# A hybrid token-mixer layer in split float32: its projections as pairs of token-major 2x2 block products in Strassen's seven-product form

## The chip, the core and the metric

The kernel runs on one core of a Trainium2 chip. The metric is the time of one execution on the device in microseconds (us), the median of three runs. TensorE multiplies (PE in the profile, PEld its weight loads), VectorE (DVE), ScalarE (ACT) and GpSimd (POOL) do the elementwise work, and SyncE (SP) issues the loads and stores.

## What is computed

The input `x` holds 512 tokens of 1024 channels, and there is one layer:

```python
h = rms_norm(x, norm_g)
y_a = spatial_gating_branch(h @ wi[:, A], ...)  # u, v, z: gelu(u) * (Ws layernorm(gelu(v)) + b) * silu(z)
y_b = moba_branch(h @ wi[:, B], ...)            # q, k, v, z: causal softmax attention, QK norm, linear bias
y_c = gla_branch(h @ wi[:, C], ...)             # q, k, v, low rank (16), z: gated linear attention
y_d = short_conv_branch(h @ wi[:, D], ...)      # b, c, x, z: b * conv3(c * x) * silu(z)
for i in range(4):
    gate = sigmoid(h @ w_merge_gate[i] + b_merge_gate[i])
    merged += gate * (y[i] @ w_branch_out[i])
x + merged @ w_out
```

Each of u, v, z, q, k and so on is 512 columns wide (in C, q and k together are). With the four gates of 1024 columns, `h` is multiplied by 22 blocks of [1024, 512]. The four branches are multiplied by [512, 1024] each and the sum by [1024, 1024].

## The kernel before

All large products keep float32 accuracy with two float32r halves of each factor (hi + lo), so a product of two [128 x 128] by [128 x 512] tiles is three matmuls into one PSUM bank (hi·hi, lo·hi, hi·lo). `h` is turned once, at the start, into the channel-major halves `hTh` and `hTl` (8 blocks of 128 channels by 512 tokens), and all of it must be there before the first product ends.

Weights arrive in blocks of 1 MB, [128 partitions x 2048], on SP's queue, in three buffers `raw` (`load`, L124). `split` (L134) makes of each half block (128x1024) a `wh` by an ACT copy (L140) and a `wl` by a DVE subtraction (L141), in three buffers each. `proj_t` (L220) gives channel-major results: for 128 channels 24 matmuls of 512 tokens (8 blocks of 128 rows, three matmuls each, L216 to L218) into one bank, from one split piece. `proj_n` (L231) gives token-major results: 96 matmuls into four banks for 512 columns (L242 to L244), from four pieces. Either way 512 columns of `h @ W` are 96 matmuls and four pieces. A branch's output product (`pb` in `merge`, L627) is 96 matmuls, and so is each half of the last projection.

The mixers (`mix_c`, `mix_b`, `mix_a`) are generators whose steps are written between the products by `run` (L285), at so many steps for every 24 matmuls; the tile framework then orders each engine's instructions by priority, with splits and the emptying of banks raised over the mixers (`PRI`). The order on an engine is fixed when the kernel is built, and each engine works through its own in order. The order of the work: C's projections, B's projections with mixer C beside them, merge of C and A's projections with mixer B beside them, merge of B with mixer A, D, merges of A and D, last projection. `s8` tiles are [128 x 2048] float32 buffers (1 MB) from a pool of 8. The low-rank columns of C take 16 matmuls (L356, L357), and four groups of four transposes each turn mixer C's output (`poT`, L487).

Of the kernel before, what the change touches and what calls it, by code (L numbers as in the profile page):

```python
# [8 lines left out]
F32 = mybir.dt.float32  # L9
# [6 lines left out]
P = 128  # L16
# [19 lines left out]
# ---- the weights as the core reads them: blocks of [128 partitions, 2048], in the order of their use  # L36
def _t_blocks(src, c0, n):
    return [(src, 0, KD, c0 + i, 256) for i in range(0, n, 256)]


def _n_blocks(src, c0):
    return [(src, r, 4, c0, 512) for r in (0, 512)]


def _merge_blocks(i, last):
    out = _t_blocks(("w_merge_gate", i), 0, D) if last else []
    for mq in range(2):
        out.append((("w_branch_out", i), 0, 4, mq * 512, 512))
        if not last:
            out += _t_blocks(("w_merge_gate", i), mq * 512, 512)  # L50
    return out


WI = ("w_in", None)
BLOCKS = (_n_blocks(WI, C_OFF + 512) + _t_blocks(WI, C_OFF, 512) + _t_blocks(WI, CZ_OFF, 512)
          + _n_blocks(WI, B_OFF) + _n_blocks(WI, B_OFF + 512) + _n_blocks(WI, B_OFF + 1024)
          + _t_blocks(WI, B_OFF + 1536, 512) + _merge_blocks(2, False)
          + _n_blocks(WI, 512) + _t_blocks(WI, 0, 512) + _t_blocks(WI, 1024, 512) + _merge_blocks(1, False)
          + [(WI, 0, KD, D_OFF + j * 512 + hf * 256, 256) for hf in range(2) for j in (1, 2, 0, 3)]
          + _merge_blocks(0, False) + _merge_blocks(3, True)  # L60
          + _n_blocks(("w_out", None), 0) + _n_blocks(("w_out", None), 512))
BLOCK_AT = {b: i for i, b in enumerate(BLOCKS)}

V_NG, V_MB, V_GB, V_QG, V_KG, V_OG, V_CW, V_CB, NVEC = 0, 8, 40, 42, 43, 44, 45, 57, 61


def lay_out(a):
    """The inputs in the order the core reads them (moves only)."""
# [3 lines left out]
    for i, ((name, sub), r, k, c, n) in enumerate(BLOCKS):  # L72
        m = a[name][0] if sub is None else a[name][0, sub]
        w[i] = m[r:r + k * P, c:c + n].reshape(k, P, n).transpose(1, 0, 2).reshape(P, k * n)
    vec = np.concatenate([a[n].reshape(-1, P) for n in ("norm_g", "b_merge_gate", "c_gate_b", "b_q_norm_g", "b_k_norm_g",
                                                        "c_out_norm_g", "d_conv_w", "d_conv_b")]).T
# [4 lines left out]
            "sb": a["a_spatial_b"][0].reshape(1, -1),  # L81
# [4 lines left out]
def hybrid_mixers(ctx: ExitStack, tc: tile.TileContext, x2, wts, lr, vec, w2, lnab, sb, swT, o2):  # L86
# [30 lines left out]
    RATE_C, RATE_B, RATE_A = 1.2, 1.5, 0.5  # L117
    WARM = 17
    PRI, FIRST = 3000, 8000

    last = {}

    # ---------------------------------------------------------------- weights
    def load(src, r, k, c, n):  # L124
        """Rows r.., columns c.. of a weight as [P, k, n]."""
        i = BLOCK_AT[src, r, k, c, n]
        raw = wp.tile([P, 2048], F32, tag="raw", name="raw")
        with tc.high_priority(offset=0 if i == 0 else PRI):
            for j in range(2 if i == 0 else 1):
                cs = slice(j * 1024, (j + 1) * 1024) if i == 0 else slice(0, 2048)  # L130
                nc.sync.dma_start(raw[:, cs], wts[i, :, cs])
        return raw.rearrange("p (k c) -> p k c", k=k)

    def split(v, sub=None, pri=PRI, pin=lambda ins: ins):  # L134
        """The two float32r halves of a [P, a, b] piece: v == hi + lo."""
        a, b = v.shape[1], v.shape[2]
        hi = wp.tile([P, 1024], F32R, tag="wh", name="wh")[:, :a * b].rearrange("p (k c) -> p k c", k=a)
        lo = wp.tile([P, 1024], F32R, tag="wl", name="wl")[:, :a * b].rearrange("p (k c) -> p k c", k=a)
        with tc.high_priority(offset=pri):
            pin(nc.scalar.copy(hi, v))  # L140
            last["lo"] = pin((sub or nc.vector).tensor_tensor(lo, v, hi.bitcast(F32), ALU.subtract))  # L141
        return hi, lo
# [18 lines left out]
    with tc.high_priority(offset=FIRST):  # L161
        for half in range(2):
# [5 lines left out]
            if half == 0:  # L168
                nc.sync.dma_start(vcol, vec)
# [61 lines left out]
    def proj_n(src, c0, xh, xl, evac, sub=None):  # L231
        """Columns c0..c0+512 of h @ src, sequence-major; evac(t, psum) for each 128 tokens."""
        banks = [bankA(f"pn{t}") for t in range(NT)]
        for kh in range(2):
            raw = None if first else load(src, 512 * kh, 4, c0, 512)
            for kq in range(2):
# [8 lines left out]
                if (kh, kq) != (1, 1):  # L245
                    yield 24
# [566 lines left out]
```

## Time and profile before

| | us |
|---|---|
| median of three runs (lowest, highest) | 700.26 (698.72, 701.78) |
| profiled execution, first to last instruction (its span) | 696.4 |
| between the span and the median | 3.9 |
| PE busy in the span | 682.4 |
| DVE, ACT, POOL busy | 336.9, 235.8, 118.9 |

An execution's own time is given for the timed runs only; of the profiled one the page gives the span. PE's busy time counts pipelined matmuls whose ends are modelled, so the pace of a stream of matmuls is read from the distance of their starts, and not from the mean length of one.

### The profile page before, as it was taken

What the parts mean: (1) busy time and instruction counts of PE and PEld (TensorE: products, weight loads), DVE (VectorE), ACT (ScalarE), POOL (GpSimd) and SP (SyncE); (2) the same over time, 40 slices, a digit from 0 to 9 for tenths busy, and PEclk for the clock granted to TensorE, in tenths of its full rate; (3) what the DMA queues carried; (4) which work ended last, traced back from release to release, by engine and by line L of the source; (5) the groups of instructions that cost most, each with busy time, mean ns of one, the idle gap of its engine ahead of it and who ended that gap; (6) DMA issues with size and microseconds to landing.
All of it is one profiled execution on the core that took longest, in us unless ns stands there. A gap on an engine that the chain in (4) does not pass through costs nothing.

```text
span 696.4 us, 7927 instructions
## 1 busy us (share of the span) xinstructions
PE 682.4 (98%) x3184; PEld 564.1 (81%) x3184; DVE 336.9 (48%) x487; ACT 235.8 (34%) x360; POOL 118.9 (17%) x141
## 2 busy tenths in 40 slices
PE   6999999999999999999999999999999999999997
PEld 5868778888788788788888888888888888888886
DVE  4426476873483446458554444444542244227711
ACT  5547423332233434344332232223132322224400
POOL 3840223352100000005631111000002211000000
PEclk9999999999999999999999999999999999999999
DMA  8314112223103031123323133223113232332131
GB/s 320 126 66 132 61 60 93 90 92 120 61 17 127 39 121 61 61 91 120 114 78 112 61 121 121 92 89 121 62 71 148 82 122 64 118 100 82 61 106 45
DMA packets 11892, 66.69 MB, mean 96 GB/s; under 512 B 1456, under 2 KB 1616, under 8 KB 4816
## 3 DMA queue, kind: packets, MB, share of 16 engines
q1 hardware_dynamic: 11856, 66.20, 26.9%
q8 instruction: 25, 0.41, 0.2%
q14 instruction: 11, 0.09, 0.0%
HBM read 64.09 MB, written 2.10 MB: 95 GB/s over the span
## 4 chain that ended last, share of the span: by engine, by line
PE 94%; DVE 2%; POOL 1%; DMA 1%; issue 1%; ACT 1%; SPq 0%; POOLq 0%; DVEq 0%
PE pt L217 11%; PE pt L218 11%; PE pt L216 11%; PE pn L242 6%; PE pn L243 6%; PE pgt L217 6%; PE pgt L216 6%; PE pn L244 6%; PE pgt L218 6%; PE pb L217 4%; PE pb L218 4%; PE pb L216 4%; PE pgr L458 2%; PE pob L603 1%; PE psc L577 1%; PE plast L783 1%
## 5 line engine op out<-in xcount | busy, mean ns | idle before, releaser
L141 DVE TENSOR_TENSOR wl<-raw,wh 128x1024 fp32r<-128x1024 f32 x104 | 133.7, 1285 | 207.5 <-ACT wh L140 192.3
L140 ACT CAST wh<-raw 128x1024 fp32r<-128x1024 f32 x108 | 113.3, 1049 | 294.0 <-PE pt L217 125.2
L216 PE MATMUL pt<-hTh,wh 128*128 128x512 f32 x352 | 137.9, 392 | 0.0
L217 PE MATMUL pt<-hTl,wh 128*128 128x512 f32 x352 | 137.2, 390 | 0.0
L218 PE MATMUL pt<-hTh,wl 128*128 128x512 f32 x352 | 137.1, 390 | 0.0
L216 PEld LDWEIGHTS pt<-hTh,wh 128*128 128x128 f32 x352 | 66.1, 188 | 14.4 <-issue 0.8
L218 PEld LDWEIGHTS pt<-hTh,wl 128*128 128x128 f32 x352 | 66.1, 188 | 13.7
L217 PEld LDWEIGHTS pt<-hTl,wh 128*128 128x128 f32 x352 | 66.1, 188 | 13.5
L216 PE MATMUL pgt<-hTh,wh 128*128 128x512 f32 x192 | 75.1, 391 | 0.0
L217 PE MATMUL pgt<-hTl,wh 128*128 128x512 f32 x192 | 74.8, 390 | 0.0
L218 PE MATMUL pgt<-hTh,wl 128*128 128x512 f32 x192 | 74.7, 389 | 0.0
L242 PE MATMUL pn<-wh,hTh 128*128 128x512 f32 x160 | 64.0, 401 | 0.0
L243 PE MATMUL pn<-wh,hTl 128*128 128x512 f32 x160 | 62.8, 392 | 0.0
L244 PE MATMUL pn<-wl,hTh 128*128 128x512 f32 x160 | 62.5, 391 | 0.0
L642 POOL TENSOR_TENSOR acc<-acc,gate 128x512 f32<-128x512 f32 x16 | 24.5, 1531 | 175.4 <-DVE gate L640 175.4
L449 POOL TENSOR_TENSOR qb<-e,qk 64x256 f32<-64x256 f32 x28 | 29.3, 1047 | 80.7 <-ACT e L444 44.5
L218 PEld LDWEIGHTS pgt<-hTh,wl 128*128 128x128 f32 x192 | 36.0, 188 | 7.5
L216 PEld LDWEIGHTS pgt<-hTh,wh 128*128 128x128 f32 x192 | 36.0, 188 | 7.4
L217 PEld LDWEIGHTS pgt<-hTl,wh 128*128 128x128 f32 x192 | 36.1, 188 | 7.4
L244 PEld LDWEIGHTS pn<-wl,hTh 128*128 128x128 f32 x160 | 30.2, 189 | 6.3
L242 PEld LDWEIGHTS pn<-wh,hTh 128*128 128x128 f32 x160 | 30.3, 189 | 6.0 <-DVE hTl L197 0.2
L243 PEld LDWEIGHTS pn<-wh,hTl 128*128 128x128 f32 x160 | 30.2, 189 | 5.7
(213 smaller groups left out, 912.8 us busy)
## 6 DMA issues: line engine op xcount, KB each, us to landing
raw<-in_w_dram SPq DMA_DIRECT2D x55, 1024.0 KB, 4.8
x<-in_x_dram SPq DMA_DIRECT2D x4, 512.0 KB, 4.9
xr<-in_x_dram SPq DMA_DIRECT2D x8, 256.0 KB, 3.5
out_dram<-xr SPq DMA_DIRECT2D x8, 256.0 KB, 2.1
raw<-in_w_dram SPq DMA_DIRECT2D x2, 512.0 KB, 8.5
lnb<-in_lnab_dram SPq DMA_DIRECT2D x1, 512.0 KB, 3.7
wsT<-in_swT_dram SPq DMA_DIRECT2D x1, 256.0 KB, 10.3
abias<-in_sb_dram SPq DMA_DIRECT2D x1, 256.0 KB, 5.0
```

What stands on the lines that cost most here:

```text
L140: pin(nc.scalar.copy(hi, v))
L141: last["lo"] = pin((sub or nc.vector).tensor_tensor(lo, v, hi.bitcast(F32), ALU.subtract))
L216: nc.tensor.matmul(ps, hi[:, k, ch], xh[:, k, :], start=(k == 0), stop=False)
L217: nc.tensor.matmul(ps, hi[:, k, ch], xl[:, k, :], start=False, stop=False)
L218: nc.tensor.matmul(ps, lo[:, k, ch], xh[:, k, :], start=False, stop=(k == kt - 1))
L242: nc.tensor.matmul(banks[t], xh[k][:, ts], hi[:, kk, :], start=(k == 0), stop=False)
L243: nc.tensor.matmul(banks[t], xl[k][:, ts], hi[:, kk, :], start=False, stop=False)
L244: nc.tensor.matmul(banks[t], xh[k][:, ts], lo[:, kk, :], start=False, stop=(k == KD - 1))
L449: nc.gpsimd.tensor_tensor(qm[hp, a].rearrange("p c (n h) -> p (c n) h", h=hh), ev[hp, :, hh:], qv[hp, :, hh:], ALU.mult)
L458: nc.tensor.matmul(pgv[:, :, c, :], e[:, c * P:(c + 1) * P], qm[:, :, c, :], start=True, stop=True)
L577: nc.tensor.matmul(psc[:, :n], qT[:, i, h * P:(h + 1) * P], kT[:, :i + 1, h * P:(h + 1) * P], start=True, stop=True)
L642: nc.gpsimd.tensor_tensor(accs[m], accs[m], g, ALU.add)
```

## The change

The 22 blocks `h @ W` are taken in 11 pairs. A pair has 1024 columns: `h` is seen as four blocks of [256 tokens x 512 channels] (A11, A12, A21, A22) and the pair's weights as four blocks of [512 rows x 512 columns], C11 and C21 of the first member and C12 and C22 of the second. `superblock` computes the four result blocks from seven block products in place of eight (Strassen's form with shared sums), each of 24 matmuls (2 groups of 128 tokens, 4 blocks of 128 channels, 3 matmuls). The products' left factors are A11, A12, A22 and four sums S1 to S4, which are made once at the start, on POOL, and split into halves. The right factors are C11, C21, C22 and four sums of weights: a block is added onto the buffer that holds another one by a DMA that accumulates (`add`), issued from POOL, once both pieces of what was in the buffer have been split. The parts that several results share are copied or subtracted out of the banks into `snap` tiles, and a result is formed from a bank and such a tile as it is emptied (`value`, and `silu2` and `gelu2` on top of it).

All results are token-major now. What must be channel-major is turned by groups of four transposes (`flip`): q and k of C, the outputs of mixers A and B, D's product before its convolution and its gate after it, and the merged sum before the last projection. The gates come ahead of the merges that use them, are written to DRAM and read back (`gd`, `gate_of`); so is A's `v` (`vd`). Their bias is added inside the superblock, on POOL and DVE. C's low-rank columns take 40 matmuls of 256 columns. Branch outputs are multiplied token-major, still 96 matmuls each. There are four buffers for `wh` and for `wl`, still three for `raw`, six `s8`. The first product starts from the first two of four token tiles.

The core of the diff, with the new functions:

```diff
-    BLOCKS: _n_blocks and _t_blocks of each projection, _merge_blocks
+BLOCKS = (_quad(WI, CQK, CV) + _quad(WI, CZ_OFF, AV)
+          + [b for i in (2, 1) for b in _quad(("w_merge_gate", i), 0, 512)]
+          + _quad(WI, BQ, BK) + _quad(WI, BV, BZ)
+          + [(("w_branch_out", 2), 0, c) for c in (0, 512)]
+          + _quad(("w_merge_gate", 0), 0, 512) + _quad(WI, AU, AZ)
+          + [(("w_branch_out", 1), 0, c) for c in (0, 512)]
+          + _quad(WI, DC, DX) + _quad(WI, DB, DZ)
+          + [(("w_branch_out", 0), 0, c) for c in (0, 512)]
+          + _quad(("w_merge_gate", 3), 0, 512)
+          + [(("w_branch_out", 3), 0, c) for c in (0, 512)]
+          + _quad(WO, 0, 512))
...
+    def add(raw, src, r, c):
+        with tc.high_priority(offset=PRI):
+            nc.gpsimd.dma_start(raw, wts[BLOCK_AT[src, r, c]], accum_op=ALU.add)
...
+        normed(0)
+        normed(1)
+        pieces1 = [split1(v4(raw1)[:, 0:2, :], 0, nc.gpsimd, pin)]
+        for blk, k0 in ((A11, 0), (A12, 4)):
+            for k in range(4):
+                p = px(0, k0 + k)
+                pin(nc.scalar.activation(blk[0][:, k, :], p, AF.Copy, scale=gk(k0 + k)))
...
+            if k0 == 0:
+                pieces1.append(split1(v4(raw1)[:, 2:4, :], 0, nc.gpsimd, pin))
+                normed(2)
+        normed(3)
...
+    def summed(blk, name, a, b, op):
+        f = s8(f"f_{name}")[:, :1024].rearrange("p (k s) -> p k s", k=4)
+        nc.gpsimd.tensor_tensor(f, a, b, op)
+        nc.scalar.copy(blk[0], f)
+        nc.vector.tensor_tensor(blk[1], f, blk[0].bitcast(F32), ALU.subtract)
+        return f
+    with tc.high_priority(offset=FIRST - 1000):
+        f1 = summed(S1, "s1", h1[:, 0:4, :], h1[:, 4:8, :], ALU.subtract)
+        for q, blk in ((0, A11), (1, A12)):
+            nc.gpsimd.tensor_tensor(h0[:, 4 * q:4 * q + 4, :], blk[0].bitcast(F32), blk[1].bitcast(F32), ALU.add)
+        f2 = summed(S2, "s2", f1, h0[:, 0:4, :], ALU.subtract)
+        summed(S4, "s4", h0[:, 4:8, :], f2, ALU.add)
+        summed(S3, "s3", h0[:, 0:4, :], h1[:, 0:4, :], ALU.subtract)
...
+    def superblock(sa, ca, sb, cb, ev, bias=None, pieces=None, raw=None):
+        c11, c21, c12, c22 = (sa, 0, ca), (sa, 512, ca), (sb, 0, cb), (sb, 512, cb)
+        def product(lhs, pcs, banks, start, after):
+            for j in range(2):
+                js = slice(j * P, (j + 1) * P)
+                for p, (hi, lo) in enumerate(pcs):
+                    for kk in range(2):
+                        k = 2 * p + kk
+                        three(banks[j], lhs[0][:, k, js], lhs[1][:, k, js], hi[:, kk, :], lo[:, kk, :],
+                              start and k == 0, k == 3)
+                emptied(after, j)
+                yield 12
...
+        r1 = raw if raw is not None else fetch(*c11)
+        yield from product(A11, pieces or split(r1), a, True, after1)
+        r3 = fetch(*c21)
+        yield from product(A12, split(r3), a, False, lambda j: ev(j, 0, a[j], ...))
+        add(r1, *c12)
+        yield from product(S1, split(r1), d, True, after5)
+        r2 = fetch(*c22)
+        add(r1, *c22)
+        yield from product(S4, split(r2), d, False, after3)
+        yield from product(S2, split(r1), b, True, lambda j: ev(j, 1, b[j], v[j], ALU.subtract))
+        add(r2, *c12)
+        yield from product(S3, split(r2), b, False, lambda j: ev(2 + j, 1, b[j], s15[j], ALU.subtract))
+        add(r1, *c21)
+        yield from product(A22, split(r1), b, False, lambda j: ev(2 + j, 0, b[j], sp1[j], ALU.add))
...
+    def flip(y, name):
+        pT = bankB(name)
+        for h in range(H):
+            nc.tensor.transpose(pT[:, h * P:(h + 1) * P], y[:, h * P:(h + 1) * P], ident)
+        return pT
...
+    run(chain(superblock(WI, CZ_OFF, WI, AV, ev_zv), gates(2), gates(1)), mixing, RATE_C)
...
+    qT, kT = v4(s8("qT")), v4(s8("kT"))
+    run(superblock(WI, BQ, WI, BK, ev_qk))
```

## Rows read from the trace of the kernel before

**Rows 1.** The page's head, busy times, chain by engine, and load queue.

```profile
span 696.4 us, 7927 instructions
PE 682.4 (98%) x3184; PEld 564.1 (81%) x3184; DVE 336.9 (48%) x487; ACT 235.8 (34%) x360; POOL 118.9 (17%) x141
...
q1 hardware_dynamic: 11856, 66.20, 26.9%
...
PE 94%; DVE 2%; POOL 1%; DMA 1%; issue 1%; ACT 1%; SPq 0%; POOLq 0%; DVEq 0%
```

**Rows 2.** Stretches: each engine's busy us (instructions), clock, DMA share, GB/s.

```profile
78.00:200.00 122.00, 118.74 (x609) 100.39 (x608) 79.00 (x129) 40.39 (x70) 38.96 (x35) 1.00 0.21 77
...
218.00:330.00 112.00, 111.91 (x560) 91.42 (x559) 61.83 (x120) 48.01 (x91) 8.60 (x11) 1.00 0.22 80
400.00:500.00 100.00, 100.00 (x446) 82.93 (x446) 45.61 (x52) 26.59 (x32) 6.25 (x6) 1.00 0.30 105
```

**Rows 3.** Timeline of PE, 430 to 436 us, first and last of 22 matmuls.

```profile
430.88 0.39 PE L216 MATMUL pt<-hTh,wh 128*128 128x512 f32 x1
...
435.64 0.39 PE L216 MATMUL pt<-hTh,wh 128*128 128x512 f32 x1
```

**Rows 4.** The chain in order of time (start, us): mixers' groups on PE.

```profile
153.91 0.89 PE pgr L458 x8
...
192.62 0.44 PE poT L487 x4
```

**Rows 5.** Groups on PE: count, then busy us, mean ns of one.

```profile
L216 PE MATMUL pt<-hTh,wh 128*128 128x512 f32 x352 | 137.9, 392 | 0.0
...
L216 PE MATMUL pgt<-hTh,wh 128*128 128x512 f32 x192 | 75.1, 391 | 0.0
...
L242 PE MATMUL pn<-wh,hTh 128*128 128x512 f32 x160 | 64.0, 401 | 0.0
```

**Rows 6.** Groups on ACT, DVE and POOL over the whole span.

```profile
L140 ACT CAST wh<-raw 128x1024 fp32r<-128x1024 f32 x108 | 113.3, 1049 | 294.0 <-PE pt L217 125.2 <-PE pgt L217 83.8 <-issue 37.0
...
L141 DVE TENSOR_TENSOR wl<-raw,wh 128x1024 fp32r<-128x1024 f32 x104 | 133.7, 1285 | 207.5 <-ACT wh L140 192.3 <-PE pm L704 5.5 <-PE pbT L553 5.1
...
L640 DVE SCALAR_TENSOR_TENSOR gate<-gate,pb 128x512 f32<-128x512 f32 x16 | 11.0, 687 | 8.3 <-PE pb L218 8.3
...
L449 POOL TENSOR_TENSOR qb<-e,qk 64x256 f32<-64x256 f32 x28 | 29.3, 1047 | 80.7 <-ACT e L444 44.5 <-PE pgr L458 21.1 <-ACT wh L140 13.9
L642 POOL TENSOR_TENSOR acc<-acc,gate 128x512 f32<-128x512 f32 x16 | 24.5, 1531 | 175.4 <-DVE gate L640 175.4
L141 POOL TENSOR_TENSOR wl<-raw,wh 128x1024 fp32r<-128x1024 f32 x4 | 9.5, 2398 | 4.8 <-ACT wh L140 4.8
```

**Rows 7.** Groups on DVE, 78 to 200 us: splits and what B's heads add.

```profile
L141 DVE TENSOR_TENSOR wl<-raw,wh 128x1024 fp32r<-128x1024 f32 x17 | 21.9, 1291 | 30.6 <-ACT wh L140 27.7 <-PE pgr L458 2.8
...
L526 DVE TENSOR_REDUCE ssb<-bsq 128x4 f32<-128x512 f32 x8 | 5.2, 675 | 0.0
```

**Rows 8.** What reads or writes `raw`: the splits' shortest, median, longest; loads' landing.

```profile
L141 DVE TENSOR_TENSOR wl<-raw,wh x104: 1209/1225/2362, 29.6 to 655.3; 128x1024 fp32r<-128x1024 f32 x104
...
DMA to landing us min/median/max: 4.6/4.8/12.8
```

**Rows 9.** Timeline of the start, 0 to 18 us, all engines.

```profile
10.95 0.89 DVE L186 TENSOR_SCALAR x<-x,rs_x 128x512 f32<-128x512 f32 x2 [0.66 <-POOL rs_x L158]
11.23 1.06 ACT L140 CAST wh<-raw 128x1024 fp32r<-128x1024 f32 x1 [0.81 <-DMA raw<-in_w_dram]
...
12.49 2.34 POOL L141 TENSOR_TENSOR wl<-raw,wh 128x1024 fp32r<-128x1024 f32 x1
12.56 2.95 DVE L186 TENSOR_SCALAR x<-x,rs_x 128x512 f32<-128x512 f32 x2 [0.67 <-POOL rs_x L158]
...
16.98 0.80 PE L242 MATMUL pn<-wh,hTh 128*128 128x512 f32 x1
```

More of the change, by code (lines that the diff above doesn't have):

```diff
@@ new lines, in hybrid_mixers @@
+    run(superblock(WI, CQK, WI, CV, ev_qkv, pieces=pieces1, raw=raw1))
+    one = cst.tile([P, 1], F32, name="one")
+    nc.gpsimd.memset(one, 1.0)
+    ind = cst.tile([P, 2], F32, name="ind")
+    nc.gpsimd.memset(ind, 0.0)
+    nc.gpsimd.memset(ind[0:64, 0:1], 1.0)
+    nc.gpsimd.memset(ind[64:128, 1:2], 1.0)
+    keep = t2("keep")
+    nc.gpsimd.memset(keep, 1.0)
+    for c in range(NT):
+        nc.gpsimd.memset(keep[:, c * P:c * P + 1], 0.0)
+    qb = []
+    for i in range(2):
+        t = cp.tile([P, 2, NT, 64], F32, name=f"qb{i}")
+        nc.gpsimd.memset(t, 0.0)
+        qb.append(t)
@@ L624, in gate @@
-    def gate(i, m, ps, g):
-        nc.scalar.activation(g, ps, AF.Tanh, bias=hmb[:, i * 8 + m:i * 8 + m + 1], scale=0.5)
-    def merge(i, ys, first=False, out=None):
-        gates = {}
-        if out is not None:
-            gs = [v4(s8("gs0")), v4(s8("gs1"))]
-            gates = {m: gs[m // 4][:, m % 4, :] for m in range(KD)}
-            yield from proj_t(("w_merge_gate", i), 0, D, lambda m, ps: gate(i, m, ps, gates[m]))
-        def ev(m, pb):
-            g = gates[m]
+        y_out(yBs, done[0], flip(done[1], "pyT"), 0.5)
@@ new lines, in hybrid_mixers, with mix_d @@
+    mixing = conv()
+    run(superblock(WI, DB, WI, DZ, ev_bz), mixing, 1.2)
+    for _ in mixing:
+        pass
+    def mix_d():
+        for t in range(NT):
+            pT = flip(bz[:, t, :], "pbz")
+            y = t2("yd")
+            nc.vector.tensor_tensor(heads(y), yD[:, :, tok(t)], heads(pT), ALU.mult)
+            y_out(yDs, t, y, 0.5)
+            yield
+    run(merge(0, yAs))
+    yDs = y_halves("D")
+    mixing = mix_d()
+    run(gates(3), mixing, RATE_D)
+    for _ in mixing:
+        pass
@@ new lines, in hybrid_mixers, with out_to @@
+    turned_m(NT - 1)
+    def out_to(t, half, ps):
+        ns = slice(half * 512, (half + 1) * 512)
+        xr = t2("xr")
+        nc.sync.dma_start(xr, x2[tok(t), ns])
+        nc.vector.scalar_tensor_tensor(xr, ps, 0.5, xr, ALU.mult, ALU.add)
+        nc.sync.dma_start(o2[tok(t), ns], xr)
+    banks = [bankA(f"po{t}") for t in range(NT)]
+    for i in range(2):
+        for p, (hi, lo) in enumerate(split(fetch(WO, i * 512, 0))):
+            for t in range(NT):
+                for kk in range(2):
+                    k = 2 * p + kk
+                    three(banks[t], mg[0][i][:, k, tok(t)], mg[1][i][:, k, tok(t)], hi[:, kk, :], lo[:, kk, :],
+                          i + k == 0, i == 1 and k == 3)
@@ new lines, in hybrid_mixers @@
+    for t in range(NT):
+        emptied(out_to, t, 0, banks[t])
+    pcs = [split(fetch(WO, i * 512, 512)) for i in range(2)]
+    for t in range(NT):
+        ps = bankA("plast")
+        for i in range(2):
+            for p, (hi, lo) in enumerate(pcs[i]):
+                for kk in range(2):
+                    k = 2 * p + kk
+                    three(ps, mg[0][i][:, k, tok(t)], mg[1][i][:, k, tok(t)], hi[:, kk, :], lo[:, kk, :],
+                          i + k == 0, i == 1 and k == 3)
+        out_to(t, 1, ps)
```

750 lines of the change are left out of this document (393 added, 357 removed).

## The prediction

> **What bounds the kernel now.** I read the page's head and chain first. PE is busy for 682.4 of 696.4 us and is 94% of the chain that ended last [rows 1]; DVE is at half, ACT at a third, POOL at a sixth, and the load queue at 26.9% of the DMA engines [rows 1]. The stretches say whether this average hides a stage with another limit: beside mixer C (78 to 200 us) PE still works 118.7 of 122 us, beside mixer B 111.9 of 112, elsewhere all of it, at the full clock of 2.4 GHz [rows 2]. But DVE's share differs: 79.0 of 122 us beside mixer C, 61.8 of 112 beside B, 45.6 of 100 elsewhere [rows 2]. So fewer PE columns shorten the kernel one for one, until another engine or a load is late; the place to look is mixer C. The profiled span of 696.4 us stands 3.9 us under the median of 700.26; I sum against the span and add 3.9. A change under 0.5% (3.5 us) can't be told from none.
>
> **Matmuls.** The pace is in the timeline: 21 matmuls of 512 columns from 430.88 to 435.64 us, 0.227 us each [rows 3]; the mean lengths near 0.39 us overlap [rows 5]. 22 blocks of 96 were 2112 matmuls (the groups of 352, 192 and 160 are one third each of their products [rows 5]). Now 11 superblocks have 7 x 24 = 168 each, 1848 in all. That is 264 fewer, x 0.227 = -59.9 us. Branch outputs and last projection stay.
>
> **Transposes.** q and k of C, y of A, y of B, the convolution's input and D's gate are turned by 4 groups each, the merged sum by 8: 28 groups of four, 0.44 us each in the chain [rows 4], +12.3 us. C's and B's other groups remain. The low-rank product goes from 16 matmuls of 512 to 40 of 256 columns: 40 x 0.114 - 16 x 0.227 = +0.9. PE's net is -46.7 us. The mixers' other matmuls keep their number and size.
>
> **The start.** Before, the first product began at 16.98 us with all of `h` turned [rows 9]. Now A11 needs two token tiles, but in the pinned order POOL subtracts the two pieces of the first weights (2.4 us each [rows 6]) between the norms. I put the first products at about 15 us, held by the second piece, and the end of the second at 28. The third needs S1: tiles 2 and 3 normed, 16 more ACT copies of about 0.5 us (half a cast [rows 6]), one POOL sum of 128x1024 (2.4), a cast (1.05), a subtraction (1.29) [rows 6], in a row from about 24: ready near 32. Five products of 5.45 us then end at 59, where seven from 16.98 would have ended at 55.1: I take +5. If POOL puts the sums of h0 first and S4 is late too, one or two more POOL sums and a cast stand in the open: +12. If S1 hides behind the first two products, the earlier start gives -2.
>
> **Splits and DVE.** A product of 24 matmuls now has two pieces to split where it had one: 14 per superblock (14.7 us of ACT, 18.0 of DVE [rows 6]) under 168 x 0.227 = 38.1 us of PE. DVE also makes four subtractions into `snap` and, per member, values out of banks: six or eight of 0.69 us (the 128x512 row of `gate` [rows 6]), so 25 to 26 us per superblock. Alone this is hidden. Beside mixer C it is tight. There three superblocks give PE 114 + about 30 of mixer (14 groups `pgr` of 0.89 [rows 4], the rest alike) = 144 us. DVE: 42 splits x 1.285 = 54; 12 subtractions and 22 values x 0.69 = 23; silu and A's `v` with its layer norm, about 20 steps x 0.69 = 14; the mixer about 52 (79.0 in the old stretch, less 21.9 of splits and about 18 for B's heads [rows 2, 7], plus some 17 steps for its gates and keys, which lay ahead of that stretch). Sum 143, so DVE is as full as PE, and in the first of the three it is over: about 57 us against 48. What slips here is the mixer. Next late are `qT` and `kT`: `vC`, `qk`, `attnT`, `szC` and the two halves of yC hold all six `s8`, so the emptying of B's q/k superblock waits for the mixer's end, and PE can run ahead by only two products. I take +6; 0 if the order lets DVE catch up, +20 if the excess of the first superblock is never made good and the mixer's last steps stand alone.
>
> The start of the trace shows what POOL does to DVE: two DVE scalings took 0.89 us, and 2.95 when they ran into a POOL subtraction of 2.34 us [rows 9]; the splits' subtractions range from 1.209 to 2.362 us, but their mean is 1.285 [rows 6, 8]. The Trainium skill (SBUF — State Buffer, "Who interferes with whom") says that a DVE instruction with two SBUF inputs, as each split's subtraction is, contends with a POOL instruction that reads SBUF, and that the second to issue waits for the whole of the first. By the rows' mean this is 6% on the splits, which the 1.285 holds already; by the rule taken at its full price, POOL's work beside mixer C (sums for the bias, layer norm, queries: some 60 us) could cost DVE up to 30 us there, for a sum near 700 us.
>
> **The accumulating DMAs.** No row shows one, and all hangs on its delay A, from when POOL could issue it to its landing. The buffer `r1` goes split, add, split, add, split, add, split through products 1, 3, 5 and 7. A split of both pieces takes 1.05 + 1.05 + 1.29 = 3.4 us [rows 6]. Four `wh` and `wl` hold two products, so the first split ends about 3 us ahead of its product; six products later (32.7 us) the fourth is wanted, its second piece 1.3 us later. So 3 A + 3 x 3.4 + 0.9 for semaphores must fit in 37.0: A up to about 8.6 us is free, each us more costs 3 us per superblock. Beside mixers C and B another 7 to 10 us of PE per superblock raise the free A to 11 or 12; that leaves six superblocks exposed. Bounds: a plain load lands in 4.8 us, the slowest took 12.8 [rows 8]. In between: 66.2 MB took 26.9% of 16 engines' 696.4 us [rows 1], so 1 MB is 3.0 us of all engines; an accumulation reads the buffer too, so I count 4.8 + 3.0, plus 1.2 for a POOL step in the way (1.05 to 1.53 [rows 6]): A = 9.0. That costs 3 x 0.4 x 6 = 7, and I take +10 for collisions: 4 adds of 6 us, 3 loads of 3 us fill 33 of 38 us of the DMA engines, the gates' trips to DRAM come on top, and behind a waiting add POOL's queries, bias sums and gelu steps wait, with DVE and the mixer's products behind those. On SP, stores of gates wait for ACT's tanh, and a fetch behind one is late by that; it is issued a product or more ahead, which covers a few us. At A = 4.8 it is 0; at 12.8 six times 12.6 and a few us in the others, +80.
>
> The Trainium skill (DMA: Bandwidth & Descriptors, "SWDGE vs HWDGE vs iDMA" and the table in "Bandwidth") says that only POOL's software path accumulates, and gives 6.15 us of transfer for a plain 1 MB load issued there; with 3.0 for the second read and 1.2 on POOL, A would be an estimated 10.4, the adds would cost about 32 us, and the time would be 697.
>
> Loads stay ahead: the next `r1` can take the buffer of `r3`, which is free after product 2's split. The last flips cost nothing while the last projection works on earlier tokens (18 matmuls, 4.1 us, against a chain of some 3); without that cover, 3.
>
> **Sum.** 696.4 - 46.7 + 5 + 6 + 10 = 670.7 us of span, 674.6 with what lies around: 675 us, 3.6% faster.
>
> **Rivals.**
> All hidden: adds within 8.6 us and DVE catching up. 696.4 - 46.7 + 0 to 5 + 3.9 = 654 to 659. For it: 79% of the load queue's time is free now, and DVE's overlap in the old stretch is real. Against: DVE as full as PE beside mixer C. Chance 0.20.
>
> Adds late (slower than before): `r1`'s chain sets the pace of the superblocks without a heavy mixer. It decides from A of about 10.5, where 3 x 1.9 x 6 = 34 us of stall, and with the start and DVE's 11, eat the 46.7. At A = 12, 61 in place of 10: 726 us. For it: DMA engines 85% full, POOL's queue in order. Against: every load but the first ones lands in about 5 us. Chance 0.27.
>
> DVE and POOL set the pace beside mixer C, and the slip goes through `qT` and `kT`: 20 to 30 in place of 6, 689 to 699 us. For it: 57 against 48 in the first superblock, the long splits [rows 8]. Against: their mean. Chance 0.11.
>
> PE doesn't gain: if a product of 24 ran slower than 24 x 0.227. Its tiles are those of L242, at the same mean [rows 5], so I give this no chance of its own.
>
> The forecast, 662 to 690, has 0.42. Faster by over 0.5%: nearly all of forecast and "all hidden", some of the rest, 0.63; within 0.5%: 0.09; slower: 0.28. The range must leave out no more than 2 in 10: from 652, the best of "all hidden", to 732, above "adds late" at A = 12.
>
> **What would show it.** 1848 + 576 matmuls of 512 columns at 0.227; 28 more groups of four transposes at 0.44; S1's product beginning near 32 us; DVE above 90% from the second superblock to B's q/k one, and PE waiting there for its evictions; the adds' landing near 8 us, with no PE wait on a split in `DC`/`DX`. An add at 11 us or more, or PE waiting for ACT's casts in each superblock with a DMA behind them, would make it wrong; so would a clock below 1.00 after stalls, which no row here prices.

## The result, and the profile after

The change made the kernel slower: 753.21 us (median of four runs, 747.61 to 758.39) against 699.49 us for the kernel before in the same session, ratio 1.0788 with a 95% interval of 1.0716 to 1.0861. The prediction was 675 us with a range to 732; the time lies above both.

The page of the changed kernel, head, queues and chain:

```profile
span 756.6 us, 8418 instructions
...
PE 681.0 (90%) x3056; PEld 547.7 (72%) x3056; DVE 487.4 (64%) x638; ACT 322.1 (43%) x455; POOL 216.2 (29%) x213
...
PEclk8868999977989999999999999999999999999999
...
q0 software_dynamic: 6336, 46.14, 32.6%
q1 hardware_dynamic: 20928, 75.36, 27.6%
...
PE 44%; DMA 12%; issue 5%; DVE 5%; ACT 2%; POOL 2%; SPq 0%; ACTq 0%; POOLq 0%; DVEq 0%
```

PE's busy time is nearly that of before [rows 1], with 128 fewer matmuls and transposes, and the clock is below full speed in the first third. The chain's shares add up to 70% only: it could be followed back no further than 220 us, so PE's 44% (94% before) says nothing of that first third. No engine is full over the whole span, so the loss must be looked for by stretch. Windows of the changed kernel (busy us, instructions; then clock, DMA share, GB/s):

```profile
20.00:40.00 20.00, 13.19 (x44) 9.50 (x44) 8.05 (x12) 9.51 (x14) 5.52 (x6) 0.83 0.61 139
40.00:60.00 20.00, 11.86 (x40) 8.31 (x40) 10.00 (x7) 7.50 (x13) 16.25 (x7) 0.66 0.38 72
60.00:80.00 20.00, 16.09 (x57) 12.84 (x58) 13.97 (x14) 7.96 (x10) 4.29 (x3) 0.83 0.43 106
89.50:149.00 59.50, 54.24 (x247) 42.21 (x245) 41.71 (x64) 32.96 (x46) 13.56 (x12) 0.97 0.59 143
149.00:228.00 79.00, 58.13 (x249) 46.66 (x248) 63.39 (x88) 29.76 (x51) 43.41 (x41) 0.85 0.47 128
228.00:287.00 59.00, 53.22 (x255) 43.83 (x254) 42.28 (x54) 26.40 (x38) 26.27 (x20) 0.94 0.62 164
287.00:330.00 43.00, 40.64 (x173) 32.08 (x172) 27.16 (x31) 21.66 (x28) 3.48 (x4) 1.00 0.76 186
500.00:560.00 60.00, 60.00 (x286) 49.75 (x285) 41.06 (x57) 21.97 (x28) 20.23 (x17) 1.00 0.59 145
```

The late stretch (500 to 560 us) is as forecast: all PE, full clock. The start (20 to 80 us) and the three superblocks beside mixer C (89.5 to 287 us) are not. (A superblock is named by its two members: CZ/AV is C's z with A's v, BQ/BK B's q with its k; "gates 2" are the gates of branch 2.) To put numbers on it I took PE's timeline from the first product of one superblock to that of the next, and counted PE's own work in each at the pace of undisturbed stretches: 0.2275 us for a product's matmul of 512 columns, 0.11 us for a tile of 128 columns (a group of four 0.44), the mixers' float32 tiles of more columns in proportion (0.43 for 512). What is left of a stretch I call its excess (waits and slow clock).

| stretch (us) | own work | excess |
|---|---|---|
| kernel before, whole | 676.8 | 13.9 |
| after, whole | 630.0 | 120.6 |
| up to the first product (2.0 to 13.1) | 5.5 | 5.6 |
| first superblock (13.1 to 89.5) | 41.3 | 35.1 |
| CZ/AV, gates 2, gates 1, beside mixer C (89.5 to 287.4) | 145.0 | 9.1 + 32.5 + 11.4 = 53.0 |
| all the rest (287.4 to 752.6) | 438.2 | 27.0 |

PE's own work did fall, by 676.8 - 630.0 = 46.8 us. Excess took 107 us. (Expectations below that quote 24.7 us for the last row count it some 2 us short.) Each excess comes from one profiled execution, of the changed kernel the slowest of its four (758.39 us), so a few us between two excesses lie within the spread of the runs.

**The start.** POOL's timeline of the changed kernel:

```profile
19.43 2.34 POOL L158 TENSOR_TENSOR wl<-raw,wh 128x1024 fp32r<-128x1024 f32 x1
22.10 1.04 POOL L150 DMA_DIRECT2D raw<-in_w_dram  x1 [0.34 <-POOL wl L158]
22.89 0.87 POOL L175 TENSOR_TENSOR rs_x<-ms_x,mhalf 128x1 f32<-128x1 f32 x1
...
34.80 0.89 POOL L150 DMA_DIRECT2D raw<-in_w_dram  x1 [10.43 <-DVE wl L158]
35.42 0.87 POOL L175 TENSOR_TENSOR rs_x<-ms_x,mhalf 128x1 f32<-128x1 f32 x1
...
44.55 2.34 POOL L243 TENSOR_TENSOR f_s<-h 128x1024 f32<-128x1024 f32 x1 [2.87 <-ACT h L237]
46.86 3.32 POOL L251 TENSOR_TENSOR h<-a11h,a11l 128x1024 f32<-128x1024 f32 x1
```

POOL is full of the mixers' masks and other constants until the second piece's subtraction at 19.43, whose cast ended at 14.9, and the first accumulating DMA goes out behind it, at 22.10. The second one waits 10.43 us at the head of POOL's queue, and the last token tile's norm (`rs_x`, 35.42), which S1 needs, stands behind it. But that norm's input was not there before 35.09 us, as ACT's and DVE's timelines show:

```profile
30.27 1.04 ACT L157 CAST wh<-raw 128x1024 fp32r<-128x1024 f32 x1 [3.23 <-DMA raw<-in_w_dram]
...
33.77 1.05 ACT L213 ACTIVATE scr<-x 128x1024 f32<-128x1024 f32 x1
...
34.94 0.15 DVE L173 TENSOR_SCALAR ms_x<-ssx 128x1 f32<-128x1 f32 x1
...
40.42 0.88 DVE L217 TENSOR_SCALAR x<-x,rs_x 128x512 f32<-128x512 f32 x2
```

On ACT the cast of the third product's weights waits until the first add has landed (30.27), and the rest of A12's halves (31.23) and the last tile's squares (33.77) stand behind that cast. So the wait on POOL delayed the norm by only some 0.3 us; the late first add and ACT's fixed order did the rest, and the tile's scaling (40.42) then stood behind two splits on DVE. The second product ended near 38, not at 28. S1's sum comes at 44.55 us and its product begins at 48.02, not near 32. PE then runs on at half speed:

```profile
48.02 1.22 PE L270 MATMUL pd<-wh,s_h 128*128 128x512 f32 x2 [3.85 <-ACT s_h L244]
51.31 0.80 PE L271 MATMUL pd<-wh,s_l 128*128 128x512 f32 x1 [2.07 <-DVE s_l L245]
51.91 0.63 PE L272 MATMUL pd<-wl,s_h 128*128 128x512 f32 x1
52.33 0.63 PE L270 MATMUL pd<-wh,s_h 128*128 128x512 f32 x1
```

Starts are 0.42 us apart, not 0.227. Windows of the same stretch give the clock:

```profile
42.00:47.90 5.90, 1.88 (x9) 1.13 (x8) 2.33 (x1) 4.48 (x9) 3.35 (x2) 0.57 0.95 178
...
50.50:53.00 2.50, 1.69 (x4) 1.40 (x5) 0.76 (x1) 0.00 (x0) 2.50 (x1) 0.50 0.00 0
```

The granted clock is 0.50, the lower level of 1.2 GHz, and PE had worked 1.88 of the 5.90 us before the product. By the distance of their starts 101 matmuls run so, 47 of them before 90 us and 36 beside mixer C; at 0.2 us each that is some 20 us of the 121.

**Beside mixer C.** In each of the mixer's 14 halving levels DVE makes `e` out of the decays `bc`, ACT takes its exponential, POOL multiplies it by the queries (`qb`), DVE by the keys (`e<-e,qk`), and PE multiplies the two (`pgr`). DVE's and POOL's groups, 89.5 to 287.4 us, changed kernel:

```profile
L560 POOL TENSOR_TENSOR qb<-e,qk 64x256 f32<-64x256 f32 x28 | 28.3, 1012 | 25.4 <-ACT e L555 21.2 <-PE pgr L569 3.0
L150 POOL DMA_DIRECT2D raw<-in_w_dram x12 | 10.6, 882 | 53.1 <-DVE wl L158 51.6 <-DVE st L544 1.5
...
L158 DVE TENSOR_TENSOR wl<-raw,wh 128x1024 fp32r<-128x1024 f32 x42 | 55.2, 1324 | 14.1 <-ACT wh L157 14.0
L553 DVE TENSOR_TENSOR e<-bc 128x512 f32<-128x512 f32 x14 | 15.5, 1121 | 0.0
...
L562 DVE TENSOR_TENSOR e<-e,qk 128x512 f32<-128x512 f32 x14 | 11.3, 806 | 12.4 <-POOL qb L560 12.1
```

DVE works 147 of 198 us there, about the 143 of the prediction, so over the whole it is not full. POOL's `qb` takes what it took before [rows 6], but POOL is now busy for 83 us, against 39 in the old stretch [rows 2]: issues of adds, bias sums, A's layer norm. `e<-bc` takes 1.12 us. Before (78 to 200 us) the same group took 0.72:

```profile
L442 DVE TENSOR_TENSOR e<-bc 128x512 f32<-128x512 f32 x14 | 9.7, 724 | 0.0
```

POOL stands 51.6 us at adds that wait for a split, with `qb` and the bias sums behind them. PE, in order, waits for the end of that chain (89.5 to 287.4 us: us, times, longest):

```profile
PE pgr L569 <- DVE e L562: 11.9, 6, 5.4
PE pd L270 <- DVE mv L675: 4.9, 1, 4.9
PE poT L366 <- POOL on L621: 3.4, 2, 3.1
```

With the smaller ones PE's waits there are 31.8 of the 53.0 us, against 3.3 in the old stretch (78 to 200 us).

**The adds.** In BQ/BK, where no mixer runs, an add into `r1` and the next one into the same buffer, and all DMA issues (KB each, median us to landing):

```profile
298.00 0.87 POOL L150 DMA_DIRECT2D raw<-in_w_dram  x1 [11.52 <-DVE wl L158]
...
310.28 0.87 POOL L150 DMA_DIRECT2D raw<-in_w_dram  x1 [7.13 <-DVE wl L158]
```

```profile
raw<-in_w_dram SPq DMA_DIRECT2D x45, 1024.0 KB, 5.6
raw<-in_w_dram POOLq DMA_DIRECT2D x44, 1024.0 KB, 8.0
```

One link of the chain add, split, add is 310.28 - 298.00 = 12.28 us, against two products of 10.9. The forecast had A + 3.4 = 12.4.

### The profile page after: what moved, and what is told of

It is laid out like the page before. It is cut to its first block, busy times and chain, and to the rows that moved or that the text cites. A ratio compares the mean times of both kernels' runs of the same rounds, so it can differ in the third digit from the quotient of the medians.

```text
span 756.6 us, 8418 instructions
## 1 busy us (share of the span) xinstructions
PE 681.0 (90%) x3056; PEld 547.7 (72%) x3056; DVE 487.4 (64%) x638; ACT 322.1 (43%) x455; POOL 216.2 (29%) x213
## 3 DMA queue, kind: packets, MB, share of 16 engines
q0 software_dynamic: 6336, 46.14, 32.6%
q1 hardware_dynamic: 20928, 75.36, 27.6%
## 4 chain that ended last, share of the span: by engine, by line
PE 44%; DMA 12%; issue 5%; DVE 5%; ACT 2%; POOL 2%; SPq 0%; ACTq 0%; POOLq 0%; DVEq 0%
DMA raw<-in_w_dram 12%; PE pb L270 4%; PE pb L271 4%; PE pb L272 4%; PE pm L270 3%; PE pm L272 3%; PE pm L271 3%; DVE wl L158 3%; PE pa L270 2%; PE pa L272 2%; PE pa L271 2%; ACT wh L157 2%; PE pd L270 1%; PE pd L272 1%; PE pd L271 1%
## 5 line engine op out<-in xcount | busy, mean ns | idle before, releaser
L158 DVE TENSOR_TENSOR wl<-raw,wh 128x1024 fp32r<-128x1024 f32 x176 | 224.4, 1281 | 141.6 <-ACT wh L157 135.6
L157 ACT CAST wh<-raw 128x1024 fp32r<-128x1024 f32 x178 | 183.6, 1047 | 193.9 <-DMA raw<-in_w_dram 73.8
L150 POOL DMA_DIRECT2D raw<-in_w_dram x44 | 38.9, 883 | 284.9 <-DVE wl L158 262.6
L270 PE MATMUL pd<-wh,s_h 128*128 128x512 f32 x176 | 74.8, 426 | 12.6 <-DVE mv L675 4.9
L270 PE MATMUL pb<-wh,s_h 128*128 128x512 f32 x176 | 73.9, 420 | 10.7 <-ACT wh L157 4.9
L271 PE MATMUL pd<-wh,s_l 128*128 128x512 f32 x176 | 72.7, 413 | 2.1 <-DVE s_l L245 2.1
L272 PE MATMUL pd<-wl,s_h 128*128 128x512 f32 x176 | 72.6, 412 | 1.0 <-DVE wl L158 0.8
L271 PE MATMUL pb<-wh,s_l 128*128 128x512 f32 x176 | 71.8, 408 | 0.0
L272 PE MATMUL pb<-wl,s_h 128*128 128x512 f32 x176 | 71.5, 406 | 0.0
L270 PEld LDWEIGHTS pd<-wh,s_h 128*128 128x128 f32 x176 | 35.1, 200 | 22.6 <-ACT e L555 5.1
L272 PEld LDWEIGHTS pd<-wl,s_h 128*128 128x128 f32 x176 | 35.1, 199 | 10.5 <-DVE wl L158 2.3
L270 PE MATMUL pa<-wh,a11h 128*128 128x512 f32 x88 | 37.0, 420 | 1.5 <-DVE a11l L229 1.5
```

The costliest lines, as they stand in the source:

```text
L150: nc.gpsimd.dma_start(raw, wts[BLOCK_AT[src, r, c]], accum_op=ALU.add)
L270: nc.tensor.matmul(ps, xh, wh, start=start, stop=False, skip_group_check=True)
L271: nc.tensor.matmul(ps, xl, wh, start=False, stop=False, skip_group_check=True)
L272: nc.tensor.matmul(ps, xh, wl, start=False, stop=stop, skip_group_check=True)
```

## The experiments

Theory 1: separate places lose the time, at first the fixed orders of the start and DVE with POOL beside mixer C, the adds being mostly covered; after adds_as_loads their chain became the third place. Theory 2, the prediction's rival: the adds land late everywhere. Excesses are counted as above. Ratios are against the kernel before, with their 95% intervals.

**adds_as_loads.** Each accumulating DMA is a plain load; leaves the weight sums out.

```diff
-            nc.gpsimd.dma_start(raw, wts[...], accum_op=ALU.add)
+            nc.sync.dma_start(raw, wts[...])
```

> Every accumulating DMA is a plain load on SP's queue into the same buffer, so the weight sums are left out. Theory 1 (fixed instruction orders at the start, and DVE with POOL beside mixer C, lose the time; the adds' own delay of about 9 us is mostly covered): no add stands in POOL's queue ahead of the norms, so the first superblock gets 10 to 20 us back, the mixer C stretch 10 at most; 725 to 745 us. Theory 2 (the adds land too late in every superblock): a load lands in about 5.6 us in place of 8 plus 0.9, the waits for weights go everywhere, under 700 us.

720.01 us, 1.0314 [1.0284, 1.0344], between the two expected ranges. Excess 82.7: first superblock 25.8 (from 35.1), mixer C 43.7 (53.0), rest 7.3 (27.0). So the adds cost 38 us of excess, about half of it outside the two other places; without them the kernel is still slower than before. Theory 2 fails as the whole cause, and theory 1 had the adds too small.

**no_levels.** Leaves out the 14 halving levels of mixer C (their steps on DVE, ACT, POOL and PE).

```diff
-            e = decayed(tau, hh, qb[i % 2])
-            if held:
-                paired(*held)
...
             yield
-        paired(*held)
```

> The 14 halving levels of mixer C are left out (its steps stay as empty steps), so the attention inside 128 tokens is missing: about 34 us of DVE, 29 of POOL, 12 of ACT and 12 of PE go, and all adds stay. Theory 1: PE's time over its own work from the second superblock to the fourth falls from 53 us to under 20; with PE's own 12 that is 700 to 715 us. Theory 2: PE's own 12 us go and the waits stay, 740 us.

722.88 us, 1.0355 [1.0239, 1.0471]. The excess beside mixer C falls from 53.0 to 37.1 only, so neither expectation holds: what is left of the mixer, with the bias sums and A's layer norm, still loses 37 us.

**start_order.** The same steps of the start on the same engines in another order: A12 emptied ahead of tiles 2 and 3, their norms ahead of the first add, h0's sums ahead of S1's, later adds and constants behind the sums.

```diff
+        with behind(rs3):
+            add(r1, *c12)
...
+        with behind(mark["s4"].ins):
+            add(r1, *c22)
```

> Only orders at the start change: A12 leaves its banks ahead of the norms of tiles 2 and 3, the norms' POOL steps stand ahead of the first add, the sums of h0 ahead of S1's, later adds and the constants of the mixers behind the sums, and the third product's split behind the copies of h1 on ACT. Theory 1: the first superblock loses 10 us in place of 35, 725 to 732 us. Theory 2: 5 us at most, since adds and their delay are as before.

752.41 us, 1.0778 [1.0726, 1.0831]; first superblock's excess 31.3, which is 4 us less, as theory 2 had it and not theory 1. Order alone is not it. Its DVE timeline shows what took the place of what the order gave:

```profile
20.62 0.88 DVE L219 TENSOR_SCALAR x<-x,rs_x 128x512 f32<-128x512 f32 x2 [0.67 <-POOL rs_x L177]
...
22.24 6.29 DVE L219 TENSOR_SCALAR x<-x,rs_x 128x512 f32<-128x512 f32 x2 [0.67 <-POOL rs_x L177]
```

POOL's two sums for h0 ran from 22.92 to 27.8 us, and two DVE scalings beside them took 6.29 us where the same two took 0.88 just before.

**gates0_beside_c.** The superblock of gates 0 goes beside mixer C too, so that the mixer's steps are spread over four superblocks.

```diff
-    run(chain(superblock(WI, CZ_OFF, WI, AV, ev_zv), gates(2), gates(1)), mixing, RATE_C)
+    run(chain(superblock(WI, CZ_OFF, WI, AV, ev_zv), gates(2), gates(1), gates(0)), mixing, RATE_C)
```

> The superblock of gates 0 moves from beside mixer B to beside mixer C, whose steps come at 0.9 in place of 1.2 for 24 matmuls (mixer B's at 1.7). Theory 1: DVE beside mixer C has four superblocks in place of three for the same steps, and 10 to 20 us come back: 735 to 745 us. Theory 2: no change within 5 us, for the adds are the same.

742.49 us, 1.0636 [1.0584, 1.0688], inside theory 1's range: the same four superblocks lose 44.1 in place of 59.1.

**start_on_dve.** The start's sums and the two first subtractions on DVE, and a new order around them.

```diff
-        nc.gpsimd.tensor_tensor(f, a, b, op)
+        nc.vector.tensor_tensor(f, a, b, op)
...
-        pieces1 = [split1(v4(raw1)[:, 0:2, :], 0, nc.gpsimd, pin)]
+        pieces1 = [split1(v4(raw1)[:, 0:2, :], 0, None, pin)]
```

> The start re-ordered and moved off POOL: the six sums that make S1 to S4 and the first two weight pieces' subtractions run on DVE; tiles 2 and 3 are normed before A12 is emptied, h0's sums stand right behind A12's halves, A12's and the first copies' evictions stand ahead of h1's, the first accumulating DMA stands behind the last norm's POOL step, the masks behind that DMA, S3 and A22 behind the splits. Nothing is left out. Theory 1 (the first superblock's excess of 35.1 us over its own PE work is made of POOL's serial steps and of what stands behind them; a POOL sum takes 2.4 to 3.3 us where DVE takes 1.3, and lengthens DVE's steps beside it): S1's product moves from 48.0 to below 32 us, the excess falls to 8 to 15 us, total 728 to 735 us. Theory 2 (the first superblock waits for its accumulating DMAs, 9 us each with little in front of them to hide behind): S1's product still waits for the first add, the excess stays above 25 us, total above 743 us.

736.01 us, 1.0556 [1.0466, 1.0645]. S1's product begins at 31.84, and the first superblock's excess is 16.1 (from 35.1), just above what was expected:

```profile
31.84 0.73 PE L274 MATMUL pd<-wh,s_h 128*128 128x512 f32 x2
33.49 0.50 PE L275 MATMUL pd<-wh,s_l 128*128 128x512 f32 x1 [0.48 <-DVE s_l L250]
```

Of the start's 35.1 us, 19 went with those steps off POOL and in the new order together; of the order alone start_order shows 4.

**adds_in_halves.** Each weight buffer as two; loads and adds of 0.5 MB, each add issued when its piece is split.

```diff
-            nc.gpsimd.dma_start(raw, wts[...], accum_op=ALU.add)
+            for p in range(2):
+                nc.gpsimd.dma_start(raw[p], wts[...][:, 1024 * p:1024 * p + 1024], accum_op=ALU.add)
```

> Every weight buffer as two buffers of half a block: each load and each accumulating DMA becomes two of 0.5 MB, and the first half's add is issued when the first piece is split, not when both are. Nothing is left out. Theory 1 (the chain split, add, split in one buffer, 12.3 us for each link in BQ/BK against 10.9 us for two products, sets the pace outside mixer C): a link becomes about 6 us for half an add and 2.3 for a split, below 10.9, so the excess outside the first superblock and mixer C falls from 24.7 us to 8 or less, the first superblock and mixer C gain some 5 to 10 together, total 725 to 735 us. Theory 2 (the DMA engines' rate sets the adds, 5.6 us of all 16 engines for each megabyte): the halves land no earlier than the whole did, and the total stays above 745 us.

728.59 us, 1.0449 [1.0360, 1.0538], inside theory 1's range; excess outside the start and mixer C 8.4 (from 27.0), BQ/BK alone 0.8 (from 4.0). Its DMA issues:

```profile
raw<-in_w_dram SPq DMA_DIRECT2D x90, 512.0 KB, 4.8
raw<-in_w_dram POOLq DMA_DIRECT2D x88, 512.0 KB, 6.5
```

A half lands in 6.5 us where the whole took 8.0, and its split is one piece of 2.3 us. The chain was the cause there, not the DMA engines' rate.

**no_pool_beside_c** and **pool_to_dve.** The first leaves out POOL's products for `qb`, the bias sums, the scale and shift of A's layer norm and the product with `szC`; the second does them on DVE.

```diff
-                nc.gpsimd.tensor_tensor(qm[hp, a]...., ev[hp, :, hh:], qv[hp, :, hh:], ALU.mult)
+                nc.vector.tensor_tensor(qm[hp, a]...., ev[hp, :, hh:], qv[hp, :, hh:], ALU.mult)
```

> Leaves out POOL's elementwise steps beside mixer C: the 28 products that fill qb, the bias sums of all gates, the scale and shift of A's layer norm, and mixer C's last product with szC. DVE keeps all its steps, and the adds stay. Theory 1a (POOL is what hurts beside mixer C: its steps lengthen DVE's, and DVE's and PE's steps wait for POOL steps that stand behind waiting adds): the excess of the three superblocks beside mixer C falls from 53 us to 25 or less, DVE's e goes from 1.12 back to about 0.69 us, total 715 to 728 us. Theory 1b (DVE's amount of work, about 143 us, and PE's fixed order of mixer steps among products set it, whoever feeds them): the excess stays above 42 us, total above 740 us.

> The POOL steps that the run before left out (28 products for qb, bias sums of all gates, scale and shift of A's layer norm, product with szC) are done on DVE; nothing is left out. DVE gets 28 x 0.35 + 20 x 0.69 = 23.6 us more beside mixer C. Theory 1a (each such step on POOL lengthens a DVE step by more than DVE would take for it, and stands behind waiting adds): the excess of the three superblocks beside mixer C falls from 53 us to 25 to 35 us, as DVE then has some 157 us of unlengthened work against 145 us of PE's own; total 728 to 738 us. Theory 1b (DVE's amount alone): the excess rises above 53 us and the total above 755 us.

Left out: 712.64 us, 1.0221 [1.0128, 1.0313], excess beside mixer C 16.8. On DVE: 726.80 us, 1.0395 [1.0351, 1.0439], excess 29.1. DVE's groups without POOL's steps (75 to 255 us):

```profile
L158 DVE TENSOR_TENSOR wl<-raw,wh 128x1024 fp32r<-128x1024 f32 x49 | 59.3, 1220 | 12.3 <-ACT wh L157 12.1
...
L556 DVE TENSOR_TENSOR e<-e,qk 128x512 f32<-128x512 f32 x14 | 9.4, 686 | 0.0
L552 DVE TENSOR_TENSOR e<-bc 128x512 f32<-128x512 f32 x14 | 9.3, 685 | 0.0
```

`e<-bc` is back from 1.12 to 0.69 us. On DVE the moved steps take 25 us beside mixer C (31 in the whole kernel), yet the kernel was 26 us faster, and DVE's busy time over the whole span rose by only 10.5 us (487.4 to 497.9): its other steps became some 20 us shorter. Theory 1a holds, and DVE's amount was not the main cause. Both runs also take POOL's steps out from behind waiting adds; adds_as_loads, which does only that and lands the weights sooner, gave 9.3 us there.

**start_halves_gates0**, **start_halves_gates0_dve**, **start_halves_gates03_dve.** The mends together: first without pool_to_dve, then with it, then with the gates of the fourth branch beside mixer C as well.

> start_on_dve, adds_in_halves and gates0_beside_c together, POOL's steps kept beside mixer C; nothing is left out. Theory 1 (three separate places, so their gains add up): excess 5 before the first product, 10 to 15 in the first superblock, 30 to 40 in four superblocks beside mixer C, 7 elsewhere, on 630 us of PE's own work: 685 to 697 us. Rival (one common cause, the DMA engines or the adds, behind all of them, so the gains overlap): above 710 us.

> The same with POOL's steps beside mixer C on DVE as well; nothing is left out. Theory 1a: four superblocks beside mixer C have some 183 us of PE's own work and 190 of DVE's, unlengthened, and lose 15 to 25 us: 672 to 687 us. Theory 1b (DVE's amount): no better than with POOL's steps, 690 us or more.

> The same with the fourth branch's gates beside mixer C too (five superblocks, the mixer's rate 0.72), and mixer D's last steps beside the merge of A; nothing is left out. Theory 1a: some 222 us of PE's own work there against 220 of DVE's, loss 8 to 15 us: 660 to 675 us. Theory 1b: 680 us or more.

718.05, 709.78 and 708.32 us, 1.0270 [1.0173, 1.0367], 1.0151 [1.0012, 1.0291] and 1.0131 [1.0087, 1.0174]: each is over 20 us above the range that theory 1 or 1a gave it and inside its rival's, so by their times alone these runs speak for the rivals. The four or five superblocks beside mixer C lose 38.3 (30 to 40 expected), 33.3 (15 to 25) and 28.1 (8 to 15), and the first superblock 26.5 to 26.8 (10 to 15), where start_on_dve alone had 16.1. POOL's timeline of the last of them points to my own order for the latter:

```profile
40.46 0.86 POOL L468 COPY mask<-m 128x256 int8<-128x256 int8 x1
41.30 2.69 POOL L152 DMA_DIRECT2D raw<-in_w_dram  x3
```

The masks fill POOL from 23.6 us on, and the second add goes out at 41.30 behind them.

**masks_behind_adds.** Five masks behind the second norm's step, the rest and the selection of mixer A's weights (`wsT`) behind the first superblock's last add.

```diff
-    cstack2.enter_context(tc.issue_after(rs3))
...
+        with tc.issue_after(rs1 if hh >= 4 else mark["add"]):
```

> start_halves_gates03_dve with POOL's own order at the start mended: five of the seven masks behind the second norm's POOL step, the other two and wsT's selection behind the first superblock's last add. In that run POOL's masks, my own placement, stood ahead of the second add and filled POOL from 23.6 to 41.3 us (the add went out at 41.3, and two products waited 7.1 and 4.0 us for what it feeds), and wsT's selection held the last norm's POOL step for 2.4 us. Nothing is left out. Theory 1 (in-order POOL ahead of the adds is what is left of the first superblock's excess): that excess falls from 26.7 to 12 us or less, total 688 to 696 us, below the kernel before. Theory 2 (the adds land too late in the first superblock whatever stands ahead of them): excess above 22 us, total above 702 us.

697.44 us, 1.0002 [0.9976, 1.0028]: level with the kernel before. The first superblock's excess is 16.2, between the two expectations: POOL's order was 10.5 us of 26.7, and the rest stayed. So this order, and no common cause, kept the first superblock's gain from adding up; the superblocks beside mixer C stay above what was expected.

**cz_av_fourth** and **best_adds_as_loads.** The superblock of CZ and A's `v`, the heaviest for DVE, fourth of the five beside mixer C; and masks_behind_adds with plain loads for adds, which leaves out the weight sums.

```diff
-    run(chain(superblock(WI, CZ_OFF, WI, AV, ev_zv), gates(2), gates(1), gates(0), gates(3)), mixing, RATE_C)
+    run(chain(gates(2), gates(1), gates(0), superblock(WI, CZ_OFF, WI, AV, ev_zv), gates(3)), mixing, RATE_C)
```

> masks_behind_adds with the superblock of CZ and A's v (the one with most DVE work: silu, gelu, layer norm) as the fourth of the five beside mixer C instead of the first. Nothing is left out. There, two stretches still lose 8.8 and 13.9 us, with DVE at 18 to 19 of 20 us from 120 to 160 us and at 13 to 17 of 20 from 260 us on. Theory 1b (DVE's amount of work in the first two superblocks, as the prediction had it for the first of three): the work is spread evenly, those two stretches lose 10 us or less together, total 684 to 692 us. Theory 1c (the mixer's serial start, decay gates, keys and states, through ACT, DVE and PE in turn, with PE in order): the loss stays with the mixer's first steps, 18 us or more, and the total within 3 us of 697.

> masks_behind_adds with each accumulating DMA as a plain load on SP's queue; leaves out the weight sums. If the adds still cost time after all (in the first superblock, 16.2 us of excess, above all): 680 to 688 us and a first superblock under 8 us of excess. If they are covered now: within 4 us of 697, and the first superblock's excess stays above 13 us.

cz_av_fourth: 693.12 us, 0.9927 [0.9901, 0.9952], 0.7% faster than the kernel before and the best complete version here, about 1 us above its expected range. Its head (of the fastest of its six runs, 689.59 us):

```profile
span 687.9 us, 8613 instructions
...
PE 655.1 (95%) x3056; PEld 530.2 (77%) x3056; DVE 501.4 (73%) x702; ACT 322.6 (47%) x455; POOL 158.8 (23%) x193
...
PEclk9999999999999999999999999999999999999999
```

The first three superblocks beside the mixer now lose 5.0 us together; CZ/AV and gates 3, where the mixer ends, lose 16.9. So the loss left the mixer's first steps (1c falls) and went with DVE's heaviest superblock, as 1b has it; the mixer's last steps lie there too now (PE waits 6.0 us for `on`), and these two were not told apart. best_adds_as_loads: 689.71 us, 0.9879 [0.9832, 0.9926], first superblock 11.3: the adds still cost some 8 us in that version, 5 of them in the first superblock, again between the two expectations.

## Why the prediction was wrong

**What held.** PE's own work fell by 46.8 us, forecast 46.7; both go by the same pace. DVE's work beside mixer C was 147 us, forecast 143. A link of the add chain was 12.28 us, forecast 12.4. These sizes were right; how much of the work hides behind PE was not.

**The failed step: DVE and POOL beside mixer C, +6 and measured 53.** The prediction compared DVE's sum with PE's and asked only what overflows. It costed DVE's steps at the rows of before, with POOL busy for 39 of 122 us, though the change itself brings POOL its bias sums, layer norm and adds there, and put POOL's effect at the 6% in the splits' mean. Moving POOL's steps to DVE took 24 of the 53 us away, leaving them out 36. DVE itself was never as full as the prediction had it: 74% of the stretch, 80% in its fullest part. The splits' mean did stay low (1.324 us); the price was paid by the mixer's own steps, and by its round trip ACT, POOL, DVE that PE waits for in order, with adds now waiting in the middle of it. The Trainium skill (SBUF — State Buffer, "Who interferes with whom"), weighed there, says that a DVE step that needs the port pair it shares with POOL, with two SBUF inputs or in a fast mode as a scaling may be, waits out a whole POOL step that was issued first. The traces agree: two scalings of 0.88 us took 6.29 beside 5 us of POOL sums. By that rule the prediction would have had 6 + 30 us lost here, nearer to the 53 than its own 6; for PE's waits in order, and for the start and the adds, it has no term.

**The start, +5 and measured some +32.** The prediction had the seven products end at 59, where the old start would have had them at 55; they end at 89.1, of which 1.8 are transposes counted elsewhere. It took S1's path as if each step began when its input was there. In the trace the queues set it: masks on POOL ahead of the second subtraction and the first add, and on ACT the cast that waits for this add (30.27) ahead of A12's halves and the last tile's squares. Of these the prediction named POOL's two subtractions alone. start_on_dve, with another engine and another order, takes 19 us away; start_order shows that the order without the engine's change is worth some 4, adds_as_loads that the add's part is 9.3.

**The adds, +10 and measured 27.0 outside the two places, 19.7 of which go with the adds.** A was right at 9.0; what was missized is the free A of 8.6 and where the rest falls. BQ/BK lost 4.0 us where 3 x 0.4 was forecast, and the last superblock with what follows it 7.7, where adds_as_loads has 1.1. Beside mixer C, where 7 to 10 us of spare PE time were to cover them, the adds cost 9.3 us, and as much in the first superblock: a late add there costs also what stands behind it, or behind its cast, in order.

**The clock, which no row of before priced.** The prediction gave it no term and named it as what could make it wrong. Some 20 us of the excess are matmuls at the lower level after such waits, so each wait of several microseconds cost more than itself. In cz_av_fourth 21 matmuls run at 0.43 us in place of 101.

The rivals: "adds late", at 726 us the nearest in time, is not the cause by itself, since plain loads leave 720. "DVE and POOL set the pace", 689 to 699, had the right place at about half of its size (20 to 30 us against 53); its path through `qT` and `kT` did not show, as BQ/BK lost 4.0 us, and 0.8 with the adds in halves. What stays open: how the three losses share the half-speed matmuls was not measured by itself; the last 16 us of the first superblock are explained by the adds for 5 only; beside mixer C the 24 us were not divided between longer DVE steps and PE's waits for the round trip, and the 17 to 29 us that stay with POOL's steps gone have no shown cause, though cz_av_fourth puts part of them with DVE's heaviest superblock.

## What to carry to other kernels

When work is taken off the engine that bounds a kernel, redo the sum for every queue that is processed in order, and ask of each instruction that can wait what stands behind it; two engines that are far from full (DVE at 74%, POOL at 42% of the stretch) are no cover for a third that waits in order for a round trip between them. Cost a DVE step from rows where the same neighbours run on POOL, and try a step on DVE before it is given to POOL to balance busy times: here 25 us of steps moved to DVE made the kernel 26 us faster. A buffer that is refilled in place is a chain; halving the unit was worth some 24 us.

## What the runs showed that was not expected

PE's clock: from 48 to 53 us, after 5.9 us in which PE worked 1.88, and from 64 to 66 us, after a wait of 4.9 us, the granted clock was 0.50 (1.2 GHz), and matmuls of 512 columns started 0.42 us apart. An accumulating DMA of 1 MB took POOL 0.88 us to issue and landed in 8.0 us (median; 13.0 at most); 46.14 MB of them took 32.6% of the DMA engines' span, where 75.36 MB of plain traffic took 27.6%: 5.6 us of all 16 engines for a block of 1 MB against 2.9 for as much plain traffic. In halves of 0.5 MB the same bytes took 35.5% and landed in 6.5 us.
